# The first stage of a transformer layer laid anew: squares from a row copy of x, rotary angles on GpSimd

## The chip, the core and the metric

The kernel runs on one core of a Trainium2 chip. A core has five engines that take instructions side by side, each from a queue of its own and in the order of that queue: TensorE (PE, matrix products; its weight loads are shown as PEld), VectorE (DVE), ScalarE (ACT), GpSimd (POOL) and SyncE (SP), which here issues transfers. DMA engines bring data from DRAM to the on-chip memory SBUF. Matrix products go to a second memory, PSUM. The metric is the time of the whole program on the device in microseconds (us), lower is better.

## What is computed

One layer with d = 1024 on 512 tokens in float32: a mixer with two kinds of attention heads, gates and an output projection, then a SwiGLU block of width 2816. What matters here is the mixer's beginning:

```
xn   = x * rsqrt(mean(x*x) + eps) * g                  # one factor per token
proj = xn @ w_in                                       # columns: q,k,v of heads A | fa cq ckv kr | gates a, b
qb   = rms_norm(cq) @ w_q_up;  kv = rms_norm(ckv) @ w_kv_up
ang  = positions * inv_freq;  cos, sin                 # rotary: turn q_rope (8 heads) and kr (shared key)
gate = sigmoid(g_ab + b_gate)
```

The factor per token, 1/rms, is applied after the projection, since it commutes with it.

## The kernel before

Every matrix product of float32 numbers is made of three products of rounded halves: `split` writes a high half (ACT: `copy`, line 101, or scaled by the gain g, line 104) and a low half (DVE: source minus high half, lines 102 and 105), and `mm3` or the job list multiplies high x high, high x low and low x high.

**Loads.** x comes transposed, in eight blocks of 128 features x 512 tokens (`xf`, letters f0 to f7 in the string at line 240). The 424 "misc" columns of w_in (fa, cq, ckv, kr) come as k0 from ACT's queue (line 176) and m0 to m3 from SP's; m0 is the second 128 rows, m1 to m3 hold 256 rows each. w0 to w2 are strips of 128 gate columns (512 KB each). `posr` (positions) and `invf` come through ACT's queue (lines 178 and 185). POOL's queue brings `c1` (identity matrix, mask), and at lines 245 to 248 the small constants `bgr` (gate bias), `tri`, `krow` and `qrow`. `bgr`, `tri` and `krow` lie in the tile `stage`, which takes one of four buffers of the tag "pt"; `rot`, the raw weight loads m2, m3 and w2, and `kvraw` take from the same four.

**The pinned stretch** (lines 323 to 344). While `pin[1]` is set, instructions on ACT and DVE keep the order of the string at line 324: f splits a block of x, k and m split misc weights, w splits a gate strip, and t squares a block of x on ACT (`sq`, line 340), with the running sum of squares on POOL (line 342). `turn(2)` after each f and `turn(1)` after each m put the next instructions of `rotary_angles` on DVE in between: 50 small instructions on 128x64 elements in all, the first of which reads the positions. The others follow at `turn(100)` (line 516). Outside pinned stretches the order on an engine is found by a scheduler that simulates the program and takes what is ready.

**PE's order** is the program's (`pin[0]`). First come 12 matmuls on zeros. Then 96 jobs of 128x424: eight steps of k, four token tiles, three products, the first six steps for all tiles in turn and the last two tile by tile. Ahead of job 72 `token_rms` sums the squares over features, and the small chain `mean4`, Ln, Exp and three products gives `rcol` (1/rms by token, tokens on partitions). After the jobs `token_rms_rows` does the same again with tokens along the row, for `rbc` (used by the gates), with two products on POOL. Then `pp` transposes the gate biases, and 33 gate matmuls (`step()`, which follows the list `stages`) cover the next chain.

**narrow** (lines 439 to 464) takes the projected columns from PSUM, sums the squares of cq and ckv on ACT and scales them on DVE into `cn`. `ptc` transposes cn, `pq` and `pqb` project it up, `rotary_key` (POOL, lines 489 to 496) turns the shared key with cos and sin, `pk` transposes the turned key, and DVE turns the queries (lines 536 to 541), which `pr` transposes. The rest of the kernel, from some 62 us on, is not touched by the change.

Of the kernel before, what the change touches and what calls it, by code (L numbers as in the profile page):

```python
# [13 lines left out]
ALU = mybir.AluOpType  # L14
# [52 lines left out]
def tile_hybrid_fox_mla_block(  # L67
# [74 lines left out]

    def rsqrt(m, n, name, out=None):

        q = small([P, n], name + "_q")
        nc.scalar.activation(out=q, in_=m, func=AF.Ln, scale=-1.0)
        nc.scalar.activation(out=q, in_=q, func=AF.Exp, scale=-0.5)
        t = small([P, n], name + "_t")
        if n == 1:
            nc.vector.scalar_tensor_tensor(out=t, in0=q, scalar=m, in1=q, op0=ALU.mult, op1=ALU.mult)  # L150
        else:
            nc.vector.tensor_tensor(out=t, in0=m, in1=q, op=ALU.mult)
            nc.vector.tensor_tensor(out=t, in0=t, in1=q, op=ALU.mult)
# [24 lines left out]
    nc.scalar.dma_start(out=posr, in_=positions.rearrange("b (t p) -> p (b t)", p=P))  # L178
# [6 lines left out]
    nc.scalar.dma_start(out=invf, in_=cst[:, C_INVF:])  # L185
# [54 lines left out]
    for ld in "f0 f1 f2 m0 f3 m1 f4 f5 m2 m3 f6 f7 w0 w1 w2".split():  # L240
        {"f": load_xf, "m": load_misc, "w": load_gate}[ld[0]](int(ld[1]))
# [29 lines left out]
    def rotary_angles():  # L271

        post = small([P, NT], "post", bufs=1)
        yield nc.vector.tensor_copy(out=post, in_=posr)
        ang, dig, q0, acc, fr = rv(0), rv(1), rv(2), rv(3), rv(4)
        yield nc.vector.tensor_tensor(
# [3 lines left out]
        for n, (unit, fa, fb) in enumerate(_turn_constants()):  # L280
            yield nc.vector.tensor_scalar(out=dig, in0=ang, scalar1=1.0 / unit, scalar2=RINT, op0=ALU.mult, op1=ALU.add)
            yield nc.vector.tensor_scalar(out=dig, in0=dig, scalar1=-RINT, scalar2=None, op0=ALU.add)
            yield nc.vector.scalar_tensor_tensor(out=ang, in0=dig, scalar=-unit, in1=ang, op0=ALU.mult, op1=ALU.add)
            yield nc.vector.tensor_scalar(out=q0, in0=dig, scalar1=fa, scalar2=RINT, op0=ALU.mult, op1=ALU.add)
            yield nc.vector.tensor_scalar(out=q0, in0=q0, scalar1=-RINT, scalar2=None, op0=ALU.add)
            yield nc.vector.scalar_tensor_tensor(out=fr, in0=dig, scalar=fa, in1=q0, op0=ALU.mult, op1=ALU.subtract)
            yield nc.vector.scalar_tensor_tensor(out=fr, in0=dig, scalar=fb, in1=fr, op0=ALU.mult, op1=ALU.add)
            if n == 0:
                yield nc.vector.tensor_copy(out=acc, in_=fr)
            else:  # L290
                yield nc.vector.tensor_tensor(out=acc, in0=acc, in1=fr, op=ALU.add)
        yield nc.vector.scalar_tensor_tensor(out=acc, in0=ang, scalar=1.0 / (2 * math.pi), in1=acc, op0=ALU.mult, op1=ALU.add)
        yield nc.vector.tensor_scalar(out=q0, in0=acc, scalar1=RINT, scalar2=None, op0=ALU.add)
        yield nc.vector.tensor_scalar(out=q0, in0=q0, scalar1=-RINT, scalar2=None, op0=ALU.add)
        yield nc.vector.tensor_tensor(out=acc, in0=acc, in1=q0, op=ALU.subtract)
# [12 lines left out]
        yield nc.vector.scalar_tensor_tensor(out=sin.rearrange(flat), in0=sh, scalar=2.0, in1=ch, op0=ALU.mult, op1=ALU.mult)
        yield nc.vector.tensor_tensor(out=q0, in0=sh, in1=sh, op=ALU.mult)
# [756 lines left out]
```

## Time and profile before

| | |
|---|---|
| median of three runs | 741.21 us (740.66 to 741.57) |
| profiled execution | 740.01 us |
| its span, first to last instruction | 738.2 us |
| PE busy | 719.0 us, 97% |
| DVE, ACT, POOL busy | 423.2, 335.4, 75.7 us |
| mean granted clock of PE, as a share of 2.4 GHz | 0.994 |

Times in the trace count from the span's start. Busy shares are means over stages of different kinds. A timeline row names start and duration, engine, line, operation, tile written and tiles read, shape, count, and in brackets the idle time ahead of the instruction with what ended it. Matmuls are pipelined, so their starts tell more than their durations. Lines are those of the kernel before; what a helper such as `split` records has the helper's line.

### The profile page before, as it was taken

Reading aid. Unit: us, or ns where it says so; the run is one execution under the profiler, and the core shown is the slowest. Engines: PE = TensorE matmul, PEld = TensorE weight load, DVE = VectorE, ACT = ScalarE, POOL = GpSimd, SP = SyncE. Lnnn points to the kernel's source line nnn. Section 1 sums busy time; section 2 is a strip of 40 time slices with the busy share of each in tenths; the row PEclk is TensorE's granted clock in tenths of the full one; section 3 lists DMA queues with packets and bytes.
Section 4 is the critical chain, followed back from the end, with each engine's and each line's share of the span. In section 5 each row is a group of like instructions: output and inputs, shape, how many; then the busy total and the mean of one; then the engine's idle time right before and its main releaser. Section 6 shows DMA issues by size and latency. Waiting matters only on the chain.

```text
span 738.2 us, 9427 instructions
## 1 busy us (share of the span) xinstructions
PE 719.0 (97%) x3553; PEld 605.8 (82%) x3553; DVE 423.2 (57%) x819; ACT 335.4 (45%) x635; POOL 75.7 (10%) x96
## 2 busy tenths in 40 slices
PE   6999899999999999999999999999999999999996
PEld 4988778989888888887898888888888888888885
DVE  6998988777998985666733333233333233225215
ACT  7457978656684874434433223232232222213113
POOL 4243441021140121200000000000000000000000
PEclk9999999999999999999999999999999999999999
DMA  8512122131322222265303332332323323223212
GB/s 284 173 34 69 44 58 59 30 87 32 113 60 61 84 57 86 86 228 172 113 1 115 86 114 86 96 105 86 112 87 93 107 86 107 94 86 113 87 58 114
DMA packets 68941, 69.45 MB, mean 94 GB/s; under 512 B 3808, under 2 KB 58352, under 8 KB 68896
## 3 DMA queue, kind: packets, MB, share of 16 engines
q1 hardware_dynamic: 66240, 64.91, 29.6%
q10 hardware_dynamic: 1824, 3.38, 1.3%
q0 software_dynamic: 832, 0.57, 0.3%
q8 instruction: 28, 0.46, 0.3%
q14 instruction: 17, 0.14, 0.1%
HBM read 66.59 MB, written 2.10 MB: 93 GB/s over the span
## 4 chain that ended last, share of the span: by engine, by line
PE 87%; DVE 6%; ACT 2%; DMA 2%; issue 2%; SPq 0%; ACTq 0%; DVEq 0%
PE pg L115 26%; PE pu L115 16%; PE pd L115 16%; PE pqa L115 6%; PE pb L115 6%; PE po L115 4%; PE pva L115 3%; PE sp L115 3%; PE py L115 3%; PE pt L120 2%; DMA wraw<-in_w_out_dram 1%; DMA wraw<-in_w_in_dram 1%; PE ptr L120 0%; DVE wol L102 0%; ACT xTh L104 0%
## 5 line engine op out<-in xcount | busy, mean ns | idle before, releaser
L102 DVE TENSOR_TENSOR wlo<-wraw,whi 128x1024 fp32r<-128x1024 f32 x102 | 125.3, 1228 | 200.1 <-ACT whi L101 199.8
L101 ACT CAST whi<-wraw 128x1024 fp32r<-128x1024 f32 x102 | 106.8, 1048 | 211.0 <-PE pu L115 78.5
L115 PE MATMUL pd<-whi,act 128*128 128x512 f32 (+1 forms) x364 | 109.2, 382 | 0.0
L115 PEld LDWEIGHTS pd<-whi,act 128*128 128x128 f32 x364 | 67.6, 188 | 13.2
L115 PE MATMUL pg<-hTh,wlo 128*128 128x512 f32 (+1 forms) x192 | 71.4, 372 | 0.0
L115 PE MATMUL pu<-hTl,whi 128*128 128x512 f32 (+1 forms) x192 | 71.3, 371 | 0.0
L115 PE MATMUL pu<-hTh,whi 128*128 128x512 f32 (+1 forms) x192 | 71.3, 371 | 0.0
L115 PE MATMUL pu<-hTh,wlo 128*128 128x512 f32 (+1 forms) x192 | 71.3, 371 | 0.0
L115 PE MATMUL pg<-hTl,whi 128*128 128x512 f32 (+1 forms) x192 | 71.3, 371 | 0.0
L115 PE MATMUL pg<-hTh,whi 128*128 128x512 f32 (+1 forms) x192 | 71.1, 371 | 0.0
L115 PE MATMUL pd<-wlo,act 128*128 128x512 f32 (+1 forms) x182 | 69.5, 382 | 0.0
L115 PE MATMUL pg<-xTh,whi 128*128 128x512 f32 x128 | 52.4, 410 | 0.0
L115 PE MATMUL pg<-xTh,wlo 128*128 128x512 f32 x128 | 50.2, 392 | 0.0
L115 PE MATMUL pg<-xTl,whi 128*128 128x512 f32 x128 | 50.0, 391 | 0.0
L115 PEld LDWEIGHTS pu<-hTh,wlo 128*128 128x128 f32 x192 | 36.2, 188 | 6.3
L115 PEld LDWEIGHTS pg<-hTh,wlo 128*128 128x128 f32 x192 | 36.2, 188 | 6.3
L115 PEld LDWEIGHTS pg<-hTh,whi 128*128 128x128 f32 x192 | 36.2, 188 | 6.3
L115 PEld LDWEIGHTS pu<-hTh,whi 128*128 128x128 f32 x192 | 36.2, 188 | 6.2
L115 PEld LDWEIGHTS pu<-hTl,whi 128*128 128x128 f32 x192 | 36.2, 188 | 6.2
L115 PEld LDWEIGHTS pg<-hTl,whi 128*128 128x128 f32 x192 | 36.2, 188 | 6.2
L115 PEld LDWEIGHTS pd<-wlo,act 128*128 128x128 f32 x182 | 34.2, 188 | 6.7
L435 POOL TENSOR_SCALAR gate<-gate 128x512 f32<-128x512 f32 x16 | 27.4, 1714 | 115.9 <-ACT gate L433 108.6
(283 smaller groups left out, 1433.0 us busy)
## 6 DMA issues: line engine op xcount, KB each, us to landing
wraw<-in_w_in_dram SPq DMA_DIRECT2D x28, 512.0 KB, 3.9
wraw<-in_w_ffn_gate_dram SPq DMA_DIRECT2D x22, 512.0 KB, 3.7
wraw<-in_w_ffn_up_dram SPq DMA_DIRECT2D x22, 512.0 KB, 3.7
wraw<-in_w_ffn_down_dram SPq DMA_DIRECT2D x22, 512.0 KB, 3.7
wraw<-in_w_out_dram SPq DMA_DIRECT2D x8, 512.0 KB, 4.2
xf<-in_xT_dram SPq DMA_DIRECT2D x8, 256.0 KB, 5.6
wraw<-in_w_branch_b_dram SPq DMA_DIRECT2D x4, 512.0 KB, 3.5
wraw<-in_w_branch_a_dram SPq DMA_DIRECT2D x4, 512.0 KB, 3.4
```

The lines of the kernel that those rows point to most:

```text
L101: one = nc.scalar.copy(out=hi, in_=src)
L102: two = nc.vector.tensor_tensor(out=lo, in0=src, in1=hi.bitcast(F32), op=ALU.subtract)
L115: ins = nc.tensor.matmul(*args, **kw)
L120: ins = nc.tensor.transpose(*args)
L435: nc.gpsimd.tensor_scalar(out=g, in0=g, scalar1=1e30, scalar2=None, op0=ALU.min)
```

## The change

Six things are done together.

1. x is loaded a second time, as four blocks of 128 token rows x 1024 (`load_rows`, r0 to r3, 512 KB each, behind w0 and w1 in SP's queue). ACT squares each row block and sums along the row (`accum_out`). The eight squares of the transposed blocks, POOL's additions and both sums by PE go.
2. `rcol` is made from these sums within the pinned stretch (entry r0 of its string, between t3 and w0). `rbc` is made by four transposes of `rcol`, broadcast along the row, and one copy by ACT. They stand ahead of job 84.
3. The rotary angles move to POOL as a whole; a fused instruction of DVE becomes two there.
4. `posr` and `invf` are loaded through POOL's queue. The issues of `bgr`, `tri`, `krow` and `qrow` stand behind the angles in the program.
5. The load string is in another order: m0 is second, m1 fifth, m2 eighth.
6. Both calls of `narrow`, the split of w2 and `split_up` are pinned, with `narrow(2, 2)` ahead of the split of w2.

```diff
+    def keep(ins):
+        if pin[1]:
+            tc.keep_in_program_order(ins)
+
     def rsqrt(m, n, name, out=None):
 
         q = small([P, n], name + "_q")
-        nc.scalar.activation(out=q, in_=m, func=AF.Ln, scale=-1.0)
-        nc.scalar.activation(out=q, in_=q, func=AF.Exp, scale=-0.5)
+        keep(nc.scalar.activation(out=q, in_=m, func=AF.Ln, scale=-1.0))
...
-    nc.scalar.dma_start(out=posr, in_=positions.rearrange("b (t p) -> p (b t)", p=P))
+    nc.gpsimd.dma_start(out=posr, in_=positions.rearrange("b (t p) -> p (b t)", p=P))
...
-    nc.scalar.dma_start(out=invf, in_=cst[:, C_INVF:])
+    nc.gpsimd.dma_start(out=invf, in_=cst[:, C_INVF:])
     c1 = big.tile([P, C_INVF], F32, name="c1", tag="c1", bufs=1)
     nc.gpsimd.dma_start(out=c1, in_=cst[:, 0:C_INVF])
...
-    sq = u8([P, 4, S], F32, "sq")
+
+    xr = [u8([P, 2, D], F32, f"xr{i}") for i in range(2)]
+    sq = xr[1].rearrange("p t (h n) -> p (t h) n", h=2)
     xf = [u8([P, 4, S], F32, f"xf{i}") for i in range(2)]
 
     def load_xf(k):
         nc.sync.dma_start(out=xf[k // 4][:, k % 4, :], in_=xT[k * P:(k + 1) * P, :])
+
+    def load_rows(t):
+        nc.sync.dma_start(out=xr[t // 2][:, t % 2, :], in_=x2[t * P:(t + 1) * P, :])
...
-    for ld in "f0 f1 f2 m0 f3 m1 f4 f5 m2 m3 f6 f7 w0 w1 w2".split():
-        {"f": load_xf, "m": load_misc, "w": load_gate}[ld[0]](int(ld[1]))
+    for ld in "f0 m0 f1 f2 m1 f3 f4 m2 f5 f6 m3 f7 w0 r0 r1 w1 r2 r3 w2".split():
+        {"f": load_xf, "m": load_misc, "w": load_gate, "r": load_rows}[ld[0]](int(ld[1]))
     nc.sync.dma_start(out=gm[:, 0:QR], in_=q_a_norm_g.broadcast_to([P, QR]))
     nc.sync.dma_start(out=gm[:, QR:QR + KVR], in_=kv_a_norm_g.broadcast_to([P, KVR]))
     nc.sync.dma_start(out=gm[:, 384:384 + NFA], in_=b_forget.broadcast_to([P, NFA]))
-    nc.gpsimd.dma_start(out=bgr, in_=b_gate.rearrange("o (m p) -> (o m) p", p=P))
-    nc.gpsimd.dma_start(out=tri, in_=cst_tri)
-    nc.gpsimd.dma_start(out=krow[96:100, :], in_=cst_rows[:, S:])
-    nc.gpsimd.dma_start(out=qrow, in_=cst_rows[:, 0:S])
...
+        tt, ts = nc.gpsimd.tensor_tensor, nc.gpsimd.tensor_scalar
+
+        def stt(out, in0, scalar, in1, op0, op1):
+            ts(out=mid, in0=in0, scalar1=scalar, scalar2=None, op0=op0)
+            tt(out=out, in0=mid, in1=in1, op=op1)
+
+        mid = rv(8)
         post = small([P, NT], "post", bufs=1)
-        yield nc.vector.tensor_copy(out=post, in_=posr)
+        nc.gpsimd.tensor_copy(out=post, in_=posr)
...
-            yield nc.vector.tensor_scalar(out=dig, in0=ang, scalar1=1.0 / unit, scalar2=RINT, op0=ALU.mult, op1=ALU.add)
-            yield nc.vector.tensor_scalar(out=dig, in0=dig, scalar1=-RINT, scalar2=None, op0=ALU.add)
-            yield nc.vector.scalar_tensor_tensor(out=ang, in0=dig, scalar=-unit, in1=ang, op0=ALU.mult, op1=ALU.add)
...
+            ts(out=dig, in0=ang, scalar1=1.0 / unit, scalar2=RINT, op0=ALU.mult, op1=ALU.add)
+            ts(out=dig, in0=dig, scalar1=-RINT, scalar2=None, op0=ALU.add)
+            stt(out=ang, in0=dig, scalar=-unit, in1=ang, op0=ALU.mult, op1=ALU.add)
+            ts(out=q0, in0=dig, scalar1=fa, scalar2=RINT, op0=ALU.mult, op1=ALU.add)
+            ts(out=q0, in0=q0, scalar1=-RINT, scalar2=None, op0=ALU.add)
+            stt(out=fr, in0=dig, scalar=fa, in1=q0, op0=ALU.mult, op1=ALU.subtract)
+            stt(out=fr, in0=dig, scalar=fb, in1=fr, op0=ALU.mult, op1=ALU.add)
...
-    angles = rotary_angles()
-
-    def turn(n):
-        for ins in (ins for _, ins in zip(range(n), angles)):
-            if pin[1]:
-                tc.keep_in_program_order(ins)
-
+        stt(out=sin.rearrange(flat), in0=sh, scalar=2.0, in1=ch, op0=ALU.mult, op1=ALU.mult)
+        tt(out=q0, in0=sh, in1=sh, op=ALU.mult)
+        ts(out=cos.rearrange(flat), in0=q0, scalar1=-2.0, scalar2=1.0, op0=ALU.mult, op1=ALU.add)
+
+    rotary_angles()
+    nc.gpsimd.dma_start(out=bgr, in_=b_gate.rearrange("o (m p) -> (o m) p", p=P))
+    nc.gpsimd.dma_start(out=tri, in_=cst_tri)
+    nc.gpsimd.dma_start(out=krow[96:100, :], in_=cst_rows[:, S:])
+    nc.gpsimd.dma_start(out=qrow, in_=cst_rows[:, 0:S])
...
+    ssx = small([P, NT], "ssx", bufs=1)
+    for st in "f0 k0 f1 k1 f2 m1 f3 f4 m2 f5 f6 m3 f7 t0 t1 t2 t3 r0 w0 w1".split():
         n = int(st[1])
         if st[0] == "k":
             split(mh[0][:, n, :], ml[0][:, n, :], mraw[0][:, n, :])
         elif st[0] == "m":
             split_misc(n)
-            turn(1)
         elif st[0] == "w":
             split_gate(n)
         elif st[0] == "f":
             split(xTh[n // 4][:, n % 4, :], xTl[n // 4][:, n % 4, :], xf[n // 4][:, n % 4, :], scale=gcol[:, n:n + 1])
-            turn(2)
+        elif st[0] == "r":
+
+            m = small([P, NT], "nx_m", bufs=1)
+            mean4(m, ssx, D)
+            rsqrt(m, NT, "nx", out=rcol)
         else:
-
-            src = xf[n // 4][:, n % 4, :]
-            dst = sq[:, 0 if n == 0 else 1 + n % 3, :]
-            tc.keep_in_program_order(nc.scalar.activation(out=dst, in_=src, func=AF.Square))
-            if n > 0:
-                nc.gpsimd.tensor_tensor(out=sq[:, 0, :], in0=sq[:, 0, :], in1=dst, op=ALU.add)
+            row = xr[n // 2][:, n % 2, :]
+            tc.keep_in_program_order(nc.scalar.activation(out=row, in_=row, func=AF.Square, accum_out=ssx[:, n:n + 1]))
...
-    ones = small([P, P], "ones", bufs=1)
-    nc.vector.memset(ones, 1.0)
-
-    def token_rms():
-        pr = bank("a", "prc")
+    def token_rms_rows():
+
+        pr = bank("a", "prb")
         for t in range(NT):
-            matmul(pr[:, t:t + 1], lhsT=sq[:, 0, t * P:(t + 1) * P], rhs=ones[:, 0:1], start=t == 0, stop=t == NT - 1)
-        m = small([P, NT], "nx_m", bufs=1)
-        mean4(m, pr[:, 0:NT], D)
-        rsqrt(m, NT, "nx", out=rcol)
-
-    def token_rms_rows():
-        pr = bank("a", "prb")
-        matmul(pr, lhsT=ones, rhs=sq[:, 0, :], start=True, stop=True)
-        m, q = tmp([P, S], "rm"), tmp([P, S], "rq")
-        mean4(m, pr, D)
-        nc.scalar.activation(out=q, in_=m, func=AF.Ln, scale=-1.0)
-        nc.scalar.activation(out=q, in_=q, func=AF.Exp, scale=-0.5)
-        nc.gpsimd.tensor_tensor(out=m, in0=m, in1=q, op=ALU.mult)
-        nc.gpsimd.tensor_tensor(out=m, in0=m, in1=q, op=ALU.mult)
-        nc.vector.scalar_tensor_tensor(out=rbc[0], in0=m, scalar=3.0, in1=q, op0=ALU.add, op1=ALU.mult)
+            transpose128(pr[:, t * P:(t + 1) * P], rcol[:, t:t + 1].broadcast_to([P, P]), ident)
+        nc.scalar.copy(out=rbc[0], in_=pr)
 
     jobs = [(t, k, p_) for k in range(6) for t in range(NT) for p_ in range(3)]
     jobs += [(t, k, p_) for t in range(NT) for k in range(6, KC) for p_ in range(3)]
     pin[0] = True
     for n, (t, k, p_) in enumerate(jobs):
-        if n == 72:
-            token_rms()
+        if n == 84:
+            token_rms_rows()
         matmul(pms[t][:, :MISCW], lhsT=xt(k, slice(t * P, (t + 1) * P))[p_ == 2],
                rhs=(mh, ml)[p_ == 1][k // 4][:, k % 4, :], start=(k, p_) == (0, 0), stop=(k, p_) == (KC - 1, 2))
-    token_rms_rows()
...
+    pin[1] = True
     narrow(0, 2)
+    narrow(2, 2)
     split_gate(2)
-    turn(100)
-    narrow(2, 2)
     split_up()
+    pin[1] = False
```

The other hunks wrap the instructions of `rsqrt`, `mean4`, `mean_rsqrt` and `narrow` in `keep(...)`, and rewrite the other lines of `rotary_angles` in the same way. The squares of `narrow` use the second row tile as scratch.

## Rows read from the trace of the kernel before

**Rows 1.** The page: busy time by engine, and one group of instructions.
```profile
PE 719.0 (97%) x3553; PEld 605.8 (82%) x3553; DVE 423.2 (57%) x819; ACT 335.4 (45%) x635; POOL 75.7 (10%) x96
...
L101 ACT CAST whi<-wraw 128x1024 fp32r<-128x1024 f32 x102 | 106.8, 1048 | 211.0 <-PE pu L115 78.5
```
**Rows 2.** Windows: length, busy PE PEld DVE ACT POOL, PEclk, DMA share, GB/s.
```profile
8.00:17.00 9.00, 6.29 (x24) 5.71 (x24) 8.72 (x12) 9.00 (x16) 6.93 (x5) 0.81 1.08 351
2.00:17.00 15.00, 10.57 (x36) 7.26 (x34) 9.47 (x13) 11.44 (x21) 7.54 (x8) 0.89 1.01 329
```
**Rows 3.** Timeline of PE: start, duration, instruction, idle before and releaser.
```profile
9.21 0.72 PE L115 MATMUL pm<-mlo,xTh 128*128 128x424 f32 x1 [2.93 <-DVE mlo L102]
...
18.84 0.46 PE L115 MATMUL pm<-mlo,xTh 128*128 128x424 f32 x1 [3.33 <-DVE mlo L102]
...
19.43 0.56 PE L115 MATMUL pm<-mhi,xTh 128*128 128x424 f32 x1
19.78 0.56 PE L115 MATMUL pm<-mlo,xTh 128*128 128x424 f32 x1
...
24.94 0.35 PE L115 MATMUL pm<-mhi,xTh 128*128 128x424 f32 x1
25.13 0.35 PE L115 MATMUL pm<-mlo,xTh 128*128 128x424 f32 x1
...
36.00 0.23 PE L120 MATMUL pp<-c,stage 16*128 16x16 f32 x1
...
56.45 0.60 PE L120 MATMUL pk<-c,rot 128*96 128x128 f32 x4
```
**Rows 4.** Timeline of DVE, first 21 us.
```profile
4.51 0.75 DVE L105 SCALAR_TENSOR_TENSOR xTl<-xf,gcol,xTh 128x512 fp32r<-128x512 f32 x1 [3.24 <-ACT xTh L104]
8.17 0.17 DVE L274 CAST post<-posr 128x4 f32<-128x4 int32 x1 [2.90 <-DMA posr<-in_positions_dram]
...
8.56 0.59 DVE L102 TENSOR_TENSOR mlo<-wraw,mhi 128x424 fp32r<-128x424 f32 x1
...
11.55 1.78 DVE L105 SCALAR_TENSOR_TENSOR xTl<-xf,gcol,xTh 128x512 fp32r<-128x512 f32 x1
...
19.70 1.03 DVE L102 TENSOR_TENSOR mlo<-wraw,mhi 128x848 fp32r<-128x848 f32 x1
```
**Rows 5.** Timeline of DVE, 30 to 33 us.
```profile
30.00 0.19 DVE L284 TENSOR_SCALAR rot<-rot 128x64 f32<-128x64 f32 x1
...
31.24 0.68 DVE L102 TENSOR_TENSOR qn<-qraw,qn 128x512 fp32r<-128x512 f32 x1
...
32.18 0.19 DVE L285 TENSOR_SCALAR rot<-rot 128x64 f32<-128x64 f32 x1
```
**Rows 6.** Timeline of POOL, up to 53 us.
```profile
9.76 7.77 POOL L342 TENSOR_TENSOR sq<-sq 128x512 f32<-128x512 f32 x5 [7.14 <-ACT sq L340]
21.03 0.55 POOL L245 DMA_DIRECT2D stage<-in_b_gate_dram  x1 [3.51 <-DVE rot L282]
...
49.41 0.33 POOL L491 TENSOR_TENSOR rot<-rot 128x64 f32<-128x64 f32 x1
49.82 0.33 POOL L492 TENSOR_TENSOR rot<-rot 128x64 f32<-128x64 f32 x1
...
50.52 1.51 POOL L435 TENSOR_SCALAR gate<-gate 128x512 f32<-128x512 f32 x1
52.12 0.34 POOL L494 TENSOR_TENSOR rot<-rot 128x64 f32<-128x64 f32 x1
```
**Rows 7.** Line L342: durations in ns (least, median, most), first and last start.
```profile
L342 POOL TENSOR_TENSOR sq<-sq x7: 1283/1312/1636, 9.8 to 24.1; 128x512 f32<-128x512 f32 x7
```
**Rows 8.** Timeline of DVE: first and last instruction of the chain to rcol.
```profile
33.22 0.15 DVE L160 TENSOR_SCALAR nx_m<-prc 128x4 f32<-128x4 f32 x1
...
35.09 0.15 DVE L155 SCALAR_TENSOR_TENSOR rcol<-nx_t,nx_q 128x4 f32<-128x4 f32 x1
```
**Rows 9.** DMA issues up to 60 us: size, median us from issue to landing.
```profile
stage<-in_b_gate_dram POOLq DMA_DIRECT2D x1, 8.0 KB, 4.0
```

More of the change, by code (lines that the diff above doesn't have):

```diff
@@ L166, in mean_rsqrt @@
         for p_ in parts[1:]:
-            nc.vector.scalar_tensor_tensor(out=m, in0=p_, scalar=-4.0 / width, in1=m, op0=ALU.mult, op1=ALU.add)
+            keep(nc.vector.scalar_tensor_tensor(out=m, in0=p_, scalar=-4.0 / width, in1=m, op0=ALU.mult, op1=ALU.add))
         return rsqrt(m, 1, name, out)
@@ L288, in rotary_angles @@
+            stt(out=ang, in0=dig, scalar=-unit, in1=ang, op0=ALU.mult, op1=ALU.add)
[3 more added lines that the diff above has]
+            stt(out=fr, in0=dig, scalar=fb, in1=fr, op0=ALU.mult, op1=ALU.add)
             if n == 0:
-                yield nc.vector.tensor_copy(out=acc, in_=fr)
+                nc.gpsimd.tensor_copy(out=acc, in_=fr)
@@ L290, in rotary_angles @@
             else:
[L291 to L295, printed above, removed]
+                tt(out=acc, in0=acc, in1=fr, op=ALU.add)
@@ L297, in rotary_angles @@
+        stt(out=acc, in0=ang, scalar=1.0 / (2 * math.pi), in1=acc, op0=ALU.mult, op1=ALU.add)
+        ts(out=q0, in0=acc, scalar1=RINT, scalar2=None, op0=ALU.add)
+        ts(out=q0, in0=q0, scalar1=-RINT, scalar2=None, op0=ALU.add)
+        tt(out=acc, in0=acc, in1=q0, op=ALU.subtract)
         t2, sh, ch = rv(5), rv(6), rv(7)
-        yield nc.vector.tensor_tensor(out=t2, in0=acc, in1=acc, op=ALU.mult)
+        tt(out=t2, in0=acc, in1=acc, op=ALU.mult)
         sc = [(-1) ** i * math.pi ** (2 * i + 1) / math.factorial(2 * i + 1) for i in range(7)]
@@ L323, in tile_hybrid_fox_mla_block @@
     pin[1] = True
-    for st in "f0 k0 f1 t0 k1 f2 t1 f3 t2 m1 t3 f4 t4 m2 t5 f5 f6 t6 f7 m3 t7 w0 w1".split():
+    ssx = small([P, NT], "ssx", bufs=1)
+    for st in "f0 k0 f1 k1 f2 m1 f3 f4 m2 f5 f6 m3 f7 t0 t1 t2 t3 r0 w0 w1".split():
         n = int(st[1])
@@ L349, in tile_hybrid_fox_mla_block @@
     pms = [bank("b", f"pm{t}") for t in range(NT)]
[L351 to L360 removed]
     def token_rms_rows():
         pr = bank("a", "prb")
[L364 to L371 removed]
+        for t in range(NT):
+            transpose128(pr[:, t * P:(t + 1) * P], rcol[:, t:t + 1].broadcast_to([P, P]), ident)
+        nc.scalar.copy(out=rbc[0], in_=pr)
     jobs = [(t, k, p_) for k in range(6) for t in range(NT) for p_ in range(3)]
@@ L446, in narrow @@
             for j, c0, c1_ in ((0, 8, 264), (1, 264, 392)):
-                nc.scalar.activation(out=jk[:, c0 - 8:c1_ - 8], in_=pms[t][:, c0:c1_], func=AF.Square, scale=rt,
-                                     accum_out=ss[:, j, t - t0:t - t0 + 1])
+                keep(nc.scalar.activation(out=jk[:, c0 - 8:c1_ - 8], in_=pms[t][:, c0:c1_], func=AF.Square, scale=rt,
+                                     accum_out=ss[:, j, t - t0:t - t0 + 1]))
         mean4(m[:, 0, :], ss[:, 0, :], QR)
@@ L452, in narrow @@
         rr = small([P, 2, n], "rr")
-        nc.vector.tensor_tensor(out=rr, in0=q, in1=rcol[:, t0:t0 + n].unsqueeze(1).broadcast_to([P, 2, n]), op=ALU.mult)
+        keep(nc.vector.tensor_tensor(out=rr, in0=q, in1=rcol[:, t0:t0 + n].unsqueeze(1).broadcast_to([P, 2, n]), op=ALU.mult))
         for t in range(t0, t0 + n):
```

43 lines of the change are left out of this document (18 added, 25 removed).

## Prediction, made before the kernel was run

> **What bounds the kernel now.** I read the page first: TensorE (PE) is busy 97% of the span [rows 1], so only a stretch in which it stands still or runs slowly can give time back. The change touches the first 60 us, so next I read windows there: from 8 to 17 us PE is busy 6.29 of 9.00 us and its granted clock is 0.81 on average, so part of that work ran at 1.2 instead of 2.4 GHz, while VectorE (DVE) is busy 8.72 and ScalarE (ACT) 9.00 us [rows 2]. Then PE's timeline: its instructions are written in a fixed order, so one late operand holds all. It waits twice for a low half of the misc weights (`mlo`, written by DVE): 2.93 us until 9.21 and 3.33 us until 18.84 [rows 3]. After such a wait the matmuls follow each other every 0.35 us (19.43, 19.78), against 0.19 later (24.94, 25.13) [rows 3]. From 18.84 on PE has work without a gap to `pp` at 36.00, its first instruction after the 96 projection matmuls.
>
> Why was `mlo` late? DVE's timeline says: twice because of the rotary angles. Its queue stood 2.90 us at `post`, which wants the positions from DRAM, with the low half of the first weights queued behind it [rows 4]. And between 10 and 18 us single DVE instructions take 1.78 us where the same shape took 0.75 at 4.51 [rows 4]; the 1.0 us more is about one addition of squares on GpSimd (POOL), 1.28 us at the least [rows 7]. The two engines exclude each other there.
>
> **The change, part by part.**
>
> *Head of PE.* With the angles gone from DVE, the low half of the first weights follows the low half of x: 4.51 + 0.75, then 0.59 [rows 4], so about 5.9 us instead of 9.15. If nothing else stops PE, 95 matmuls at 0.19 end at 5.9 + 18.1 = 24.0, and the four transposes that spread 1/rms cost about what the four of `pk` cost, 0.60 [rows 3]: `pp` at 24.6, against 36.00. The old path (eight one-column matmuls and a 128x512 pair over the squares) goes, so nothing else is added on PE. The second weights now load second, not fourth, and the third (`m1`) fifth; I take them as in time, since each step of k costs PE 12 x 0.19 = 2.3 us and 3 us of slack come from the next term anyway.
>
> *The row loads and rcol.* The transposes stand before matmul 84 and wait for `rcol`, which waits for all four row blocks: this wait is new, and 12 matmuls, `pp` and all gates are queued behind it. Ahead of the last row block the queues hold 2.10 MB of xT, 1.74 of misc weights, 1.05 of the first two gate strips, 2.10 of rows and some 0.15 of small things: 7.14 MB. From 2 to 17 us the transfers ran at 329 GB/s, from 8 to 17 at 351 [rows 2]. By the second, 2.0 + 20.3 = 22.3 us; by the first, 23.7. I take the second, since larger lines move in the rows. One square of 128x1024 on ACT costs about the 1.05 of a cast of that shape [rows 1] and 0.2 for its sum (an estimate): 23.6. The chain from the mean to `rcol` took 33.22 to 35.24 [rows 8], 2.0 us, among other work; six instructions like the two shown would add up to some 1.0 alone (an estimate). I take 2.0: `rcol` at 25.6, with 22.6 to 27 as bounds. PE reaches matmul 84 at 5.9 + 83 x 0.19 = 21.7 and stands 3.9 us; that is longer than the two waits above, so I price the 12 matmuls at 0.35: 25.6 + 0.6 + 4.2 = 30.4 for `pp`. Gain there 36.0 - 30.4 = 5.6 us, and 9.7 were the rows in time.
>
> The gate strips' splits stand behind that on ACT and DVE (two casts of 1.05 and their low halves): done near 29, in time for `pp`. `narrow` may start when `rcol` is there, since its first two banks are complete before matmul 84. It is hidden by 33 gate matmuls as before; pinning its instructions costs nothing while those cover it.
>
> *The eight squares by ACT and seven sums by POOL* go: 8 x 0.6 us of ACT and 7 x 1.3 of POOL, all off PE's path once it waits for rows instead.
>
> *The angles on POOL.* Counted in the code: 72 instructions of 128x64 (a fused DVE instruction becomes two), each fed by the one before. The nearest rows are POOL's own 128x64 products in `rotary_key`: L491 starts 0.41 before L492 [rows 6]. Its bounds are 0.33 (the duration alone) and 0.45; I take 0.40, so 28.8 us. They start when the positions have landed: at best 4.0 us [rows 9] after an issue in the first 2 us, so 6, at worst at 8.17, when they landed before [rows 4]; I take 7.0. While they run, DVE has low halves to compute that read two SBUF operands: in the head nine left (six of 0.75, three of 1.03) = 7.6 us, the strips 3 x 1.3 and `split_up` some 3.4 (by 0.68 for 512 columns [rows 5]): 14.9 us together. What does POOL lose by that? Five additions took 7.77 us [rows 6] where 5 x 1.28 = 6.4 would do [rows 7], while DVE had one low half of 0.59, two of 0.75 and four angle instructions of some 0.2 in that time, 2.9 us of own work: a share of 0.48. So 7.1 us here. With four DMA issues of 0.55 and two gate minima of 1.5 among them [rows 6], the angles end at 7.0 + 28.8 + 7.1 + 2.2 + 3.0 = 48.1, and the eight instructions of `rotary_key`, two of them twice as wide, need 3.6 more at 0.45: 51.7 us.
>
> Who waits for that? The transposes `pk`, in PE's order at 56.45 [rows 3], now at 56.45 - 5.6 = 50.85. So a new stall of 0.9, and the gain is capped at 56.45 - 51.7 = 4.7 us however early the rows come. The products with sine and cosine on DVE need the angles at about 48 as well; PE wants those only after `pk`, at `pr`, so I give them no price here (the last rival does).
>
> The Trainium skill speaks against this part: "GPSIMD Engine Reference", section 4.1, sends elementwise work to VectorE and gives GpSimd about twice the time for two inputs. The rows agree in direction (0.34 for 128x64 on POOL [rows 6], 0.19 for an angle instruction on DVE [rows 5]), and the cost above already holds it.
>
> *bgr, tri, krow, qrow.* Their issues now stand behind the angles in the program. `bgr` feeds `pp`, and everything on PE is queued behind `pp`. The order on POOL isn't the program's: this scheduler fills the gap of a dependent chain with a later instruction that is ready. On DVE a split of `split_up` went between L284 and L285 of the angles, though it stands later in the program [rows 5]; on POOL a gate's minimum (L435) went ahead of L494 [rows 6]. And `stage` gets its space only when an earlier load has been split (the issue waited until 21.03 [rows 6]; the low half of `m2`, whose buffer it can take, began on DVE at 19.70 and took 1.03 [rows 4]). So I expect `bgr` in the middle of the angles, issued at 17 to 30 us, landed 4.0 later [rows 9]: mostly ahead of 30.4.
>
> *Sum.* 36.0 - 30.4 = 5.6 saved, 0.9 given back at `pk`: 4.7. After that PE's order and work are as before, and the weights for it have queue to spare. The profiled execution took 740.01 us (span 738.2), so 735.3; the median of the runs is 1.2 above it (741.21), so I forecast a median of **736.5**, with 733 to 740 as this case's own range.
>
> **The rivals.**
>
> *POOL and the rows both quick* (chance 0.15). If POOL's chain runs at 0.33 it ends 5.0 us sooner, with `pk` at 46.7, and if `rcol` comes at its early bound, 22.6, the wait at matmul 84 is 0.9 us, shorter than either wait after which the pitch rose. `pp` then comes at 22.6 + 0.6 + 2.3 = 25.5, 10.5 early, of which `pk` lets 9.7 through: 741.2 - 9.7 = 731.5; with half of the one or the other, 733. I say 732. For it: the rows have 4 KB lines. Against: the gate strips with 512-byte lines lie among them.
>
> *The lock takes all* (0.13). DVE's rows show it standing for a whole POOL instruction [rows 4]. If POOL stands for the whole of DVE's too, it loses 14.9, not 7.1: `kr3` at 59.5, so `pk` 3.0 later than before, and the time is 744. For it: DVE's share of the rows; against: the 0.48 counted above. The change would then not do what it says, since DVE's freed time comes back as POOL's. The Trainium skill states this rule on its page ("SBUF — State Buffer", section "SBUF: two separate sides": an exclusive lock for the whole instruction, on which the other side fully blocks); the trace agrees for DVE and only half for POOL.
>
> *bgr behind the angles* (0.15). If the four issues stay in program order, `bgr` is issued at 7.0 + 28.8 + 7.1 = 42.9 and lands at 46.9; `pp` then stands 10.9 later than its old 36.0, and the time is 752. It decides from an issue later than 32.0, where it eats the whole gain. For it: the program's order; against: the fillings named above.
>
> *Given back later* (0.09): sine and cosine late hold DVE's queue with the low halves of `cq` behind them, and PE loses what it won: 741.
>
> **How the numbers follow.** The forecast has 0.48, the four rivals 0.52. About 0.2% (1.5 us) is what a measurement of this kernel can tell from no change. Faster: 0.48 without a tail of 0.01, and 0.15, so 0.62. Same: 0.09 with small tails of forecast and lock, 0.13. Slower: 0.15 and most of the lock's 0.13 with a tail, 0.25. The range reaches from the quick rival to past the lock, 731.5 to 746, and leaves out mainly `bgr` behind the angles.
>
> **What would show it.** Right: second matmul of PE near 6 us, no wait for `mlo` over 1 us, a wait of 2 to 5 us at the new transposes with ScalarE's row squares or their load as the releaser, `pp` between 29 and 32, POOL's angles ending between 42 and 50, `pk` near 51. Wrong: `pp` waiting for a DMA of POOL (the third rival), `pk` waiting for POOL past 55 (the second), or PE already throttled before matmul 84. The forecast falls with any of: rows later than 27 us, POOL's pitch over 0.5, `bgr` issued after 32.

## The result, and the profile after

The changed kernel took 749.14 us (median of four runs, 746.32 to 750.27) beside 740.93 (739.61 to 741.57) for the kernel before in the same comparison: a ratio of 1.0107, interval 1.0076 to 1.0139. It is slower, where 736.5 was forecast. The profiled execution took 750.27 us, its span 748.5.

Line numbers from here on are those of the changed kernel, or of the experiment that is named. First the windows that answer to [rows 2], with the same columns.

```profile
8.00:17.00 9.00, 8.20 (x42) 7.33 (x41) 7.63 (x11) 6.66 (x10) 8.24 (x14) 1.00 1.05 400
2.00:17.00 15.00, 14.20 (x62) 10.87 (x61) 9.52 (x13) 9.10 (x15) 10.27 (x19) 1.00 1.00 349
```

In the head the change does what it says: PE is busy 8.20 of 9.00 us where it was 6.29, at full clock. PE's timeline (start, duration, instruction, idle before and releaser) shows the rest, to be read against [rows 3].

```profile
5.77 0.54 PE L115 MATMUL pm<-mhi,xTh 128*128 128x424 f32 x1
6.14 0.35 PE L115 MATMUL pm<-mlo,xTh 128*128 128x424 f32 x1
...
11.99 0.46 PE L115 MATMUL pm<-mlo,xTh 128*128 128x424 f32 x1 [0.55 <-DVE mlo L102]
...
23.50 0.62 PE L120 MATMUL prb<-c,rcol 128*128 128x128 f32 x4
31.34 0.28 PE L120 MATMUL pp<-c,stage 16*128 16x16 f32 x1 [4.89 <-DMA stage<-in_b_gate_dram]
...
55.76 1.65 PE L115 MATMUL pq<-upw,cq 128*128 128x256 f32 x6 [6.21 <-DVE kvs L102]
...
62.78 0.60 PE L120 MATMUL pk<-c,rot 128*96 128x128 f32 x4
```

The two waits for `mlo` are gone, and the transposes of `rcol` stand at 23.50 with hardly a wait. But `pp` waits 4.89 us for a constant from DRAM, and `pq`, which waited for nothing before, stands 6.21. `pp` is 4.7 us earlier than before and `pk` 6.3 later. What holds `pq` is seen on ACT's timeline:

```profile
32.25 0.61 ACT L514 CAST krs<-stage 4x512 fp32r<-4x512 f32 x1 [4.08 <-DMA stage<-in_cst_rows_dram]
...
46.18 1.05 ACT L101 CAST whi<-wraw 128x1024 fp32r<-128x1024 f32 x1
53.94 0.63 ACT L429 ACTIVATE gate<-gate 128x512 f32<-128x512 f32 x1 [6.71 <-POOL gate L428]
...
55.13 0.75 ACT L101 CAST kvs<-ptc 128x128 fp32r<-128x128 f32 x4
```

From 47.2 to 53.94 ACT stands at the gate's logarithm (L429), which wants the gate's minimum from POOL. Behind it in ACT's queue are the casts of `kvs` (the high halves of the ckv columns that `ptc` transposed). These casts and the low halves that DVE makes after them are the last readers of the PSUM banks (the parts of PSUM that a product is written to) of `ptc`, and `pq` gets its bank when those are read. POOL's timeline says why the minimum is late:

```profile
7.10 0.19 POOL L286 CAST post<-posr 128x4 f32<-128x4 int32 x1 [3.61 <-DMA posr<-in_positions_dram]
...
25.72 0.58 POOL L325 DMA_DIRECT2D stage<-in_b_gate_dram  x1 [0.16 <-issue]
...
42.89 3.88 POOL L317 TENSOR_SCALAR rot<-rot 128x64 f32<-128x64 f32 x1
46.73 1.92 POOL L281 TENSOR_SCALAR rot<-rot 128x64 f32<-128x64 f32 x1
48.73 0.33 POOL L282 TENSOR_TENSOR rot<-rot 128x64 f32<-128x64 f32 x1
49.14 0.32 POOL L482 TENSOR_TENSOR rot<-rot 128x64 f32<-128x64 f32 x1
...
52.41 1.49 POOL L428 TENSOR_SCALAR gate<-gate 128x512 f32<-128x512 f32 x1
```

The angles run from 7.10 to 49.06, six products of the rotary key follow, and only then comes the minimum. The issue of `bgr` is in the middle of the angles, at 25.72, and landed 5.6 us later (the view of DMA issues from 20 to 45 us, against the 4.0 of [rows 9]):

```profile
stage<-in_b_gate_dram POOLq DMA_DIRECT2D x1, 8.0 KB, 5.6
```

The two long waits cost more than their length: PE came out of both at half rate. In these windows of the changed kernel (columns as above) the granted clock is 0.50 of 2.4 GHz after `pp` and after `pq`; in the kernel before the same stretch had none of it.

```profile
30.00:36.00 6.00, 4.66 (x12) 3.65 (x13) 0.61 (x4) 3.46 (x13) 4.83 (x15) 0.50 0.58 167
36.00:42.00 6.00, 6.00 (x30) 4.96 (x29) 5.24 (x24) 4.50 (x16) 5.01 (x16) 0.97 0.01 3
55.70:60.00 4.30, 4.24 (x16) 3.95 (x17) 3.53 (x20) 2.19 (x6) 1.49 (x1) 0.50 0.00 0
```

So from `pp` to `pk` the kernel needs 31.4 us in place of 20.4: 7.0 of waits at `pq` (6.2, and 0.8 for `cq`), and half of 4.66 + 4.24 us of busy time, 4.4, through the clock; together 11.4 (an estimate), against 11.0 seen.

That is not all. PE's starts at six points of the two traces (us from the span's start; `pu` and `pd` are the up and down products of the feed-forward stage):

| | pp | pk | last score product | first pu | first pd | last pd |
|---|---|---|---|---|---|---|
| before | 36.0 | 56.5 | 274.2 | 376.5 | 611.4 | 731.1 |
| after | 31.3 | 62.8 | 279.8 | 381.7 | 618.5 | 741.5 |
| after - before | -4.7 | +6.3 | +5.6 | +5.2 | +7.1 | +10.4 |

Half of the loss arises in the feed-forward stage, 320 us after the last line that was edited. PE doesn't wait there; its matmuls take longer. The groups of instructions from 400 to 735 us (busy us, mean ns of one), two of the kernel before:

```profile
L115 PE MATMUL pd<-wlo,act 128*128 128x512 f32 x170 | 66.1, 389 | 0.0
L115 PE MATMUL pu<-hTh,wlo 128*128 128x512 f32 x160 | 62.2, 389 | 0.0
```

All its groups of this shape stand at 389. The same ones and two more of the kernel after:

```profile
L115 PE MATMUL pd<-wlo,act 128*128 128x512 f32 x167 | 66.0, 395 | 0.0
L115 PE MATMUL pu<-hTh,wlo 128*128 128x512 f32 x160 | 63.0, 394 | 0.0
L115 PE MATMUL pu<-hTl,whi 128*128 128x512 f32 x160 | 62.7, 392 | 0.0
...
L115 PE MATMUL pu<-hTh,whi 128*128 128x512 f32 x160 | 62.1, 388 | 0.0
```

### The profile page after: what moved, and what is told of

The parts are those of the page before. It is cut to its first block, busy times and chain, and to the rows that moved or that the text cites. A ratio compares the mean times of both kernels' runs of the same rounds, so it can differ in the third digit from the quotient of the medians.

```text
span 748.5 us, 9425 instructions
## 1 busy us (share of the span) xinstructions
PE 724.0 (97%) x3547; PEld 605.1 (81%) x3547; DVE 406.8 (54%) x766; ACT 336.5 (45%) x634; POOL 99.2 (13%) x161
## 4 chain that ended last, share of the span: by engine, by line
PE 82%; DVE 8%; DMA 3%; POOL 3%; ACT 2%; issue 2%; DVEq 0%; POOLq 0%
PE pg L115 23%; PE pu L115 16%; PE pd L115 15%; PE pqa L115 6%; PE pb L115 6%; PE po L115 4%; PE pva L115 3%; PE sp L115 3%; PE py L115 3%; PE pt L120 2%; DMA wraw<-in_w_out_dram 1%; DMA stage<-in_cst_rows_dram 1%; DVE wlo L102 1%; DMA rot<-in_cst_dram 1%; DVE hb L105 1%
## 5 line engine op out<-in xcount | busy, mean ns | idle before, releaser
L115 PE MATMUL pd<-whi,act 128*128 128x512 f32 (+1 forms) x364 | 111.2, 388 | 0.0
L115 PE MATMUL pg<-xTh,whi 128*128 128x512 f32 x128 | 54.1, 422 | 0.0
```

The source lines that it names most:

```text
L115: ins = nc.tensor.matmul(*args, **kw)
```

## The experiments

Two theories of the first stage: A, the gate minimum behind the angles decides, and what is won ahead of it is waited out at `pq`; B, the late `bgr` decides, since all of PE is queued behind `pp`. And one of the feed-forward stage, L: the weight tiles lie elsewhere. In the built programs they begin at byte 202,624 of a partition in place of 202,432, because four small tiles (`ssx`, `nx_m`, `nx_q`, `nx_t`: 32 + 32 + 64 + 64 bytes) are now first used ahead of them. Modulo 512 that is 384 in place of 192; the other large tiles that PE reads are at 192 in both. Ratios are against the kernel before, run beside each; its median in these comparisons was 740.93 to 741.72 us, so times from different comparisons can be set side by side to about 1 us.

**Constants ahead of the angles** (`e1_const_early`).

```diff
-    rotary_angles()
     nc.gpsimd.dma_start(out=bgr, ...)                  # a tile of its own
     nc.gpsimd.dma_start(out=tri, in_=cst_tri)
     nc.gpsimd.dma_start(out=krow, ...)                 # krow = yfa[64:68, 2, :]
     nc.gpsimd.dma_start(out=qrow, ...)
+    rotary_angles()
...
     split_up()
+    keep(nc.scalar.copy(out=krs[96:100, :], in_=krow))
```

> Constants without the wait: `bgr` gets a buffer of its own and `krow` a free corner of `yfa`, their four issues stand ahead of the angles, and the copy of `krow` follows `split_up` on ACT. Theory A (the loss is ACT waiting for a gate's minimum that stands behind the angles on POOL): `pp` moves from 31.3 to about 26, but `pq` still waits for the release of its PSUM bank until some 55 us, `pk` stays near 62, time 747 to 750 as for the change. Theory B (the loss is the late constants): `pp` at 26, all after it 5 us earlier, `pk` near 57 to 58, time 744.

752.14 us, ratio 1.0144 (1.0108 to 1.0180). `pp` came at 25.7, 5.6 earlier, and `pk` at 63.5, later than ever. The waits from 20 to 75 us (total, times, longest):

```profile
PE pq L115 <- DVE kvs L102: 12.5, 1, 12.5
```

```profile
ACT gate L430 <- POOL gate L429: 14.0, 2, 12.5
```

All that was won at `pp` is waited out at `pq`: with `bgr` in time PE only comes to the gates' late minimum sooner. B by itself falls. (The edit does two things, `bgr` sooner and the copy of `krow` later on ACT; no run separates them.)

**The gate minimum on VectorE** (`e2_min_on_dve`).

```diff
-        nc.gpsimd.tensor_scalar(out=g, in0=g, scalar1=1e30, scalar2=None, op0=ALU.min)
+        nc.vector.tensor_scalar(out=g, in0=g, scalar1=1e30, scalar2=None, op0=ALU.min)
```

> The change with one edit: the minimum of each gate runs on DVE, not POOL. Theory A: ACT's wait of 6.7 us for POOL goes, `pq` waits under 2 us, `pk` comes when the turned key is ready on POOL, 53 to 56, so 6 to 8 us before the change: time 741 to 743. Theory B: `pp` still at 31.3 and no gain behind it: 749.

749.03 us, ratio 1.0099 (1.0061 to 1.0138). PE's waits from 20 to 75 us:

```profile
PE pp L120 <- DMA stage<-in_b_gate_dram: 5.4, 1, 5.4
PE pq L115 <- DVE cq L102: 2.8, 1, 2.8
PE pq L115 <- DVE kvs L102: 2.4, 1, 2.4
```

`pq` waits 2.4 in place of 6.2 us for `kvs`, but 2.8 in place of 0.8 for `cq`, and `pp` still waits 5.4 for `bgr`. `pk` comes at 60.2, 2.6 earlier; by the end of the score products 2.3 of that are gone again, and the median is that of the changed kernel. So A by itself falls too: alone, neither edit is worth anything.

**Both** (`e3_both`): the two diffs above together.

> Both edits of the two runs above. Theory A with POOL as the next bound: `pp` at 26, `pk` not before the turned key, 53 to 55, so no more than 2 us better than with the minimum on DVE alone: 740 to 742. Theory B, or both losses adding up: 735 to 738.

743.78 us, ratio 1.0031 (1.0016 to 1.0046), 5.4 us less than the changed kernel. `pp` 26.0, `pk` 54.0: 2.4 us *ahead* of the kernel before. A and B (the late constants, `krow` among them) name two delays on one path, and mending them pays only together. Yet the kernel is still slower than before, by what the feed-forward stage loses (matmuls at 388 to 396 ns as above). One new wait shows:

```profile
DVE qra L532 <- POOL rot L283: 2.3, 1, 2.3
```

Sine and cosine, still on POOL, hold DVE's queue for 2.3 us.

**The angles back on VectorE** (`e4_angles_on_dve`), in two blocks:

```diff
-    for st in "f0 k0 f1 k1 f2 m1 f3 f4 m2 f5 f6 m3 f7 t0 t1 t2 t3 r0 w0 w1".split():
+    for st in "f0 k0 f1 k1 f2 m1 f3 f4 m2 f5 f6 m3 f7 a0 t0 t1 t2 t3 r0 a1 w0 w1".split():
...
+        elif st[0] == "a":
+            turn((28, 100)[n])                         # steps of the angles, on nc.vector
```

> The change with its third part undone: the 50 angle instructions run on DVE, 28 of them pinned where DVE waits for the rows, the rest ahead of the gate strips; rows, load order and transposes as in the change. If all losses come from POOL's chain: `pp` at 26 to 27, `pk` 9 us earlier than in the kernel before, near 47, time 731 to 734. If the second load of x or the pinned order of `narrow` is what costs: 741 or more.

748.34 us, ratio 1.0104 (1.0073 to 1.0135). A miss, from a wait that the edit made itself:

```profile
PE pg L115 <- DVE wlo L102: 6.4, 1, 6.4
```

The tail of the angles on DVE stood ahead of the gate strips' low halves. So that place on DVE is no better for the angles than POOL; whether another would be, this run doesn't show.

**Addresses alone, in the kernel before** (`e5_before_shifted`).

```diff
+    small([P, 40], "pad", bufs=1)                      # 160 bytes, never touched
+    nx_m = small([P, NT], "nx_m", bufs=1)              # 32 bytes, else allocated later
     shift = small([P, 112], "shift", bufs=1)
```

> The kernel before, nothing moved but addresses: 192 bytes are put ahead of the split weight tiles (a pad of 160 and the mean's tile, allocated early), so that they stand at the kernel after's offset, 202624 in place of 202432, while everything else stays. Theory L (the slower feed-forward stage of the kernel after comes from where its weight tiles lie): matmul of hTh,whi about 388, of hTl,whi 392, of hTh,wlo 394 and of the down projection 395 ns in place of 389, the feed-forward stage some 5 us longer, first stage as before, 746. Rival (it comes from the first stage, by way of the transfers' timing or of other tiles): groups at 389 ns, 741.

746.14 us, ratio 1.0061 (1.0042 to 1.0079): 4.4 us slower with every instruction as before. Its groups:

```profile
L115 PE MATMUL pd<-wlo,act 128*128 128x512 f32 x170 | 67.2, 395 | 0.0
L115 PE MATMUL pu<-hTh,wlo 128*128 128x512 f32 x160 | 63.0, 394 | 0.0
L115 PE MATMUL pu<-hTl,whi 128*128 128x512 f32 x160 | 62.7, 392 | 0.0
L115 PE MATMUL pu<-hTh,whi 128*128 128x512 f32 x160 | 62.1, 388 | 0.0
```

Nanosecond for nanosecond those of the kernel after. Of the operands of these matmuls only the weight tiles moved. L holds. From the first `pu` to the last `pd` the traces give 354.6 us before, 359.8 here and 359.8 in the kernel after: 5.2 us, free of what the first stage does.

**Addresses alone, in the kernel after** (`e6_after_shifted`).

```diff
+    small([P, 80], "pad", bufs=1)                      # 320 bytes; 32, 96 and 16 in the runs below
     shift = small([P, 112], "shift", bufs=1)
```

> The kernel after, nothing moved but addresses: a pad of 320 bytes brings the split weight tiles to the offset modulo 512 that they had before (192). Theory L: all groups of the feed-forward stage at 389 ns, pk still at 62.8 us, 5 us less in all, 744. Rival: 749, groups at 392 to 396 ns.

745.28 us, ratio 1.0061 (1.0042 to 1.0080), 3.9 less than without the pad (some 4.6 when each is taken against the kernel before in its own comparison); all groups at 389; `pk` still at 61.9. What the first stage alone costs is what remains: 3.6 us by the medians, 4.5 by the ratio.

**Which addresses** (`e10_after_offset0`, `e11_after_offset256`, `e12_after_offset448`: pads of 128, 384 and 64 bytes in the kernel after).

> The kernel after with a pad of 128 bytes: the split weight tiles at offset 0 modulo 512, all other large tiles at 192. If a tile has only to be clear of some bad offset, or to be aligned: groups of the feed-forward stage at 389 ns, 745. If the weights have to lie at the same offset as the tiles that stream against them: 392 to 396 ns as at 384, 749.

> The kernel after with a pad of 384 bytes: the split weight tiles at offset 256 modulo 512. If the offset has to be the one of the streaming tiles: 392 to 396 ns, 749. If alignment to 256 bytes or nearness to 192 is enough: 389 ns, 745.

> The kernel after with a pad of 64 bytes: the split weight tiles at offset 448 modulo 512, an odd multiple of 64 as 192 is, while 0, 256 and 384 (all slower) are multiples of 128. If the weights have to lie at the streaming tiles' own offset modulo 512 (192): 391 to 396 ns, 749 to 753. If an odd multiple of 64 is enough: 389 ns in all groups, 745.

| weight tiles modulo 512 | 192 | 448 | 384 | 256 | 0 |
|---|---|---|---|---|---|
| us | 745.28 | 744.30 | 749.14 | 753.29 | 753.87 |
| ratio | 1.0061 | 1.0034 | 1.0107 | 1.0156 | 1.0171 |
| first `pu` to last `pd`, us | 354.7 | 354.7 | 359.8 | 361.8 | 361.8 |

The groups of the first fence are of offset 0, those of the second of 448:

```profile
L115 PE MATMUL pd<-wlo,act 128*128 128x512 f32 x162 | 63.5, 392 | 0.0
...
L115 PE MATMUL pu<-hTh,wlo 128*128 128x512 f32 x160 | 63.3, 396 | 0.0
```

```profile
L115 PE MATMUL pd<-wlo,act 128*128 128x512 f32 x170 | 66.1, 389 | 0.0
...
L115 PE MATMUL pu<-hTh,wlo 128*128 128x512 f32 x160 | 62.2, 389 | 0.0
```

The two odd multiples of 64 are fast, the three multiples of 128 slow, so it isn't alignment to a larger power of two and isn't equality with the other tiles' 192 modulo 512. Whether 192 and 448 are good in themselves, or only beside tiles at 192, was not tried: no run moved those.

**First stage mended and addresses restored** (`e7_both_shifted`), on top of `e3_both`:

```diff
-    bgr = small([16, P], "bgr", bufs=1)
+    bgr = yfa[0:16, 2, 0:P]
...
+    small([P, 80], "pad", bufs=1)
```

> Constants ahead of the angles and the gate minimum on VectorE as in the run of both edits, with the same pad of 320 bytes (and the gate biases in the spare rows of another tile in place of a tile of their own). Theory (first stage and addresses are two separate losses that add): pk at 54.0, feed-forward groups at 389 ns, 738.5 to 739.5, faster than before. If the addresses are not the cause: 743.8.

738.90 us, ratio 0.9970 (0.9958 to 0.9982): faster than the kernel before. The two losses are separate and add up: the address is worth 4.9 here (743.78 to 738.90), 3.9 and 4.4 above; the order 6.4 (745.28 to 738.90), 5.4 above.

**The angles shared** (`e8_angles_shared`), on top of the last, with a0 ahead of t0 in the pinned string:

```diff
+        elif st[0] == "a":
+            for _, ins in zip(range(28), angles):      # on nc.vector
+                tc.keep_in_program_order(ins)
+            on[0] = nc.gpsimd
+            for _ in angles:                           # the rest
+                pass
```

> As the run before it, and the first 28 steps of the angles on VectorE, in its idle time ahead of the row sums, the rest on GpSimd. If it is only sine and cosine at 49 us that hold VectorE there (2.3 us at 49.4): sine and cosine by 41, rotary key by 45, no stand of VectorE for them, pk at 51.7, 736 to 737. If the minima, the casts or the eviction set pk: 54, 738.5 to 739.5.

738.76 us, ratio 0.9965 (0.9953 to 0.9976); `pk` 53.7 in place of 54.3. A miss by about 2 us. DVE no longer waits for sine and cosine, but POOL ended the angles at 44.4, not 41, because of one row:

```profile
37.91 6.10 POOL L285 TENSOR_SCALAR rot<-rot 128x64 f32<-128x64 f32 x2
```

and PE still waits at `pq` in both, 5.0 us in `e7_both_shifted` (2.6 for `cq`, 2.4 for `kvs`) and 4.6 here. After these waits the clock falls; the window of `e7_both_shifted` around them:

```profile
45.00:51.50 6.50, 4.90 (x18) 4.42 (x19) 2.79 (x10) 0.95 (x2) 5.49 (x15) 0.55 0.47 127
```

**Up projections split after the transposes** (`e9_up_after_features`), on top of the last, to have `cq` sooner:

```diff
-    split_up()
+    split_rope()                                       # only the two pairs that pq needs
...
     for t in range(NT):
         step()
         narrow_to_features(t)
+    split_up()                                         # the other four, not pinned
```

> As the run of the shared angles, and of the up projections' splits only the rotary columns stand ahead of the narrow projection's transposes; the other five pairs follow them. If VectorE's order is what holds pq there (2.2 us for cq and 2.4 for kvs, behind 5.5 us of low halves at 37.8 to 43.4): cq's low half by 40, no wait at pq, pk at 49 to 50, 734 to 736 if the pairs that now come later hold nobody. If they do hold the first heads (qn and kvs feed them), or if VectorE is simply full from 35.9 to 54: pk earlier and sp no earlier, 738 to 739.

740.41 us, ratio 0.9987 (0.9975 to 0.9999): a miss. `pq` waits 1.3 for `cq` and 3.0 for `kvs`, and `pk` is at 55.7. The splits that were no longer pinned were put in between by the scheduler, one of them even ahead of `narrow`. What the waits at `pq` hang on stays open. The trace of `e7_both_shifted` gives a hint:

```profile
42.96 1.40 DVE L102 TENSOR_TENSOR cq<-ptc,cq 128x256 fp32r<-128x256 f32 x4
```

ACT had written the high halves of `cq` by 40.84; their low halves began on DVE only 2.1 us later, behind low halves and other work that keep DVE without a gap from 37.10 on. That DVE is simply full there is a guess that no run settles.

**Later gate minima back on GpSimd** (`e13_shared_min_early` on top of `e8_angles_shared`, `e14_both_min_early` on top of `e7_both_shifted`):

```diff
-        nc.vector.tensor_scalar(out=g, ...)
+        (nc.vector if m in early else nc.gpsimd).tensor_scalar(out=g, ...)
```

> As the run of the shared angles, and only the four early gates' minima on VectorE; the twelve later ones on GpSimd as before. If moving the later minima costs the 2 us between pk and the end of the attention loop: no PE wait on ptl, pk 53.7 and sp's end 270.5, 736.5 to 737.5. If the later stretch doesn't depend on them: 738.8.

> As the run of both edits with the pad of 320 bytes (angles wholly on GpSimd), and only the four early gates' minima on VectorE. If the later minima cost 2 us: pk 54.3, sp's end 272, 737 to 738. If not: 738.9. Against the other kernel of this call it also prices the sharing of the angles again: 0.6 us by pk.

739.08 (ratio 0.9962, 0.9948 to 0.9976) and 738.99 (0.9960, 0.9944 to 0.9977): no change from 738.76 and 738.90. The wait on `ptl` did go, others came in its place, and the time stayed. So moving these minima does not give the last 2 us.

## Why the prediction was wrong

*Head of PE: right.* Second matmul at 6.1 (5.9 forecast), no wait for `mlo` over 0.55, full clock from 8 to 17 us.

*Row loads and rcol: right in kind, too dear.* The chain to `rcol` began on DVE at 21.94 and ended at 23.39, against 25.6 forecast, within the bounds of 22.6 to 27. The rate was as reckoned (349 GB/s from 2 to 17 us; the sum took 351). What the sum had wrong is the order of the loads. It put 1.05 MB of two gate strips ahead of the last row block, as the program does, but in SP's queue all four row blocks stand ahead of both strips:

```profile
9.92 2.83 SPq L212 DMA_DIRECT2D xr<-in_x_dram  x4
13.10 0.38 SPq L235 DMA_DIRECT2D wraw<-in_w_in_dram  x1
```

By its own rate that is 3.0 us less; ACT had the last block at 20.75, 1.6 sooner than the 22.3 forecast. And the chain took 1.4 us, not 2.0. PE stood hardly at matmul 84, so the price for a lower clock there fell away too: where `bgr` was early, `pp` came at 25.7 to 26.0, not at 30.4.

*bgr: right in part.* It was issued in the middle of the angles as argued, at 25.7, inside the 17 to 30 given. But it landed 5.6 us later, not 4.0, and as the rows had come sooner, it was `bgr` that set `pp`, at 31.3. The forecast of 30.4 was nearly met by luck, with a mistake on either side.

*Angles on POOL: the end was met, in part by luck.* They ended at 49.06 (48.1 forecast). But the sum had two gate minima, 3.0 us, ahead of that end, and none ran there: the first began at 52.41. Without them the sum gives 45.1. The 72 instructions, with what they lost to DVE, took 39.7 us (7.10 to 49.06 less four issues), not 35.9. Undisturbed they followed each other every 0.435 us (starts at 41.16, 41.62 and 42.03 on POOL's timeline), not 0.40: 31.3 us, which leaves some 8.4 for DVE's share where 7.1 was reckoned (both are estimates; the share of 0.48 is 0.47 by its own terms). In time this share lies in lumps, 3.88 and 1.92 us, while DVE computes low halves. The last product of the key ended at 52.33; then the gate minimum took its turn, and the key was whole at 54.5 (51.7 forecast).

*Who waits for POOL: the step that failed.* The prediction asked only for `pk`, and reckoned the gate minima as 3.0 us *on POOL's* account. It had itself shown that a minimum takes its turn on POOL between rotary products [rows 6], and did not ask who is queued behind whoever waits for it: ACT's logarithm, behind that the casts of `kvs`, behind these PSUM banks and `pq`. The rival of things given back later had the mechanism, a queue held with operands of PE behind, on the wrong engine (DVE, for sine and cosine; that wait is there too, 2.3 us in `e3_both`, once the first is gone). The same question missed the copy of `krow`, which the scheduler put ahead of `narrow` on ACT, where it stood 4.08 us for its load. Price of the step, together with the late `bgr`, since neither pays alone: 5.4 us by `e3_both`, 6.4 by `e7_both_shifted` against `e6_after_shifted`.

*A wait's second price.* The prediction charged a lower clock to the wait for rows and none to a wait behind it. In the changed kernel some 4.4 us of the 11.0 lost between `pp` and `pk` are clock, by the windows above.

*"After that PE's order and work are as before": failed as well.* Order and count of the instructions are as before, their duration isn't. The edit's small tiles moved the weight tiles by 192 bytes, which costs 3.9 to 4.9 us of the medians in four comparisons (`e5_before_shifted`, `e6_after_shifted`, `e12_after_offset448` and `e7_both_shifted` against `e3_both`), and 5.2 us of the feed-forward stage in the traces. No row of before could have told the price; that the tiles move could be seen in the code.

*The sum.* 749.1 - 736.5 = 12.6. About 4 to 5 are the addresses and 5.4 to 6.4 the order on POOL and ACT, depending on which is mended first. The remaining 2.4 (738.9 against 736.5) lie ahead of `pk`, which came at 54.3 in `e7_both_shifted` where 51.7 was forecast: the waits of 5.0 at `pq` with the lower clock after them eat the 4.5 us by which `pp` came sooner than forecast and 2.6 more. What these waits hang on is not settled; two tries to shorten the way to `pk` failed (`e8_angles_shared`, `e9_up_after_features`). The prediction had `narrow` and what is pinned with it hidden by the gate matmuls, at no price. That is not borne out: PE stood 0.45 us in all from 20 to 75 us in the kernel before, and stands at `pq` for 3 us and more in every kernel with the change. Whether the pinning does it or the order, no run separates. The main idea, that PE's head gives back some 5 us, is borne out only where both losses are mended, and there 2.8 us are left of it.

*The rivals.* `bgr` behind the angles and the lock taking all were wrong in their mechanism, though the result lies between their times (752, 744). One sign that the prediction named for the first of them did show, `pp` waiting for a DMA of POOL, but after an issue at 25.7, not behind the angles.

## What to carry to other kernels

When work moves to another engine, ask of every instruction already queued there who waits for it, and what is queued behind that waiter, until the chain ends at the engine that bounds the kernel; the price is set by the last in that chain. Two delays on one path hide each other: mending one alone may show nothing or a loss, so try them together before giving up either. And compare the mean duration of one and the same instruction in a stage that was not edited: if it changed, look at where the tiles lie before looking for a wait.

## What was not expected of the hardware

*The place of a weight tile changes the pace of matmuls.* A 128x512 matmul took 389 ns with the weight tiles at 192 or 448 modulo 512 bytes, 388 to 396 at 384, and 391 to 396 at 0 and 256; between the best and the worst, 9.6 us of this kernel (744.30 and 753.87), 7.1 of them in the feed-forward stage. The Trainium skill, "SBUF — State Buffer", section "Who interferes with whom", says that PE never waits on anyone and that the port pair of VectorE and GpSimd is the only place of contention. The runs here show a cost on PE that depends on addresses alone, so the measurement decides; by what mechanism, they don't show.

*GpSimd was passed over several times in a row.* The 128x64 instruction at 42.89 takes 0.37 us elsewhere and took 3.88. DVE's timeline in that time:

```profile
42.81 1.22 DVE L102 TENSOR_TENSOR wlo<-wraw,whi 128x1024 fp32r<-128x1024 f32 x1
43.94 0.68 DVE L102 TENSOR_TENSOR qn<-qraw,qn 128x512 fp32r<-128x512 f32 x1
...
45.82 0.68 DVE L102 TENSOR_TENSOR kvs<-wraw,kvs 128x512 fp32r<-128x512 f32 x1
46.42 0.26 DVE L748 SCALAR_TENSOR_TENSOR rot<-rot 128x32 f32<-128x32 f32 x1
...
48.34 1.40 DVE L102 TENSOR_TENSOR cq<-ptc,cq 128x256 fp32r<-128x256 f32 x4
```

Six low halves with both inputs in SBUF follow each other, and POOL gets on only near 46.4, when DVE turns to something small; its next instruction is held again until DVE turns to `cq`, whose one input is in PSUM. The Trainium skill, "SBUF — State Buffer", section "SBUF: two separate sides", has the lock for a whole instruction and, under "Who interferes with whom", the exception for one SBUF input; the trace agrees with both. Here the lock was also not handed over between two low halves that follow at once. It isn't so everywhere: DVE was busy without a gap from 10.86 to 17.55 us too, and no instruction that POOL began in that time took longer than 1.26. There each low half of the weights (TENSOR_TENSOR) is followed by one or two of x (SCALAR_TENSOR_TENSOR, the operation of the small instruction at 46.42 as well). Whether that is what lets POOL in, no run shows.
